# A squared-ReLU MLP on one core: the gate's squares taken from reloaded sums, a third result buffer, and operand builds due by their load

## The chip, the cores and the metric

The kernel runs on one core of one Trainium2 chip. The metric is the device time of one execution in microseconds (us), shown as the median of several runs. TensorE (PE) multiplies, VectorE (DVE) and ScalarE (ACT) work on elements, GpSimd (POOL) and SyncE (SP) mostly issue DMA transfers here. Each engine executes its own instructions in the order in which the program emits them, and waits where an instruction needs something that is not ready.

## The reference

One decoder layer on 512 prompt rows and 64 sample rows (8 sequences of 8), 576 rows in all; D_MODEL is 2048, D_FF 8192. An input projection feeds attention and a convolution, whose outputs go through an output projection; then the second part, which the change is about:

```python
def finish_layer(x, attn, conv_y, pe, g_attn_out, w_out, g_mlp, w_up, w_down, g_ple, w_ple, w_ple_gate):
    B, L = x.shape[0], x.shape[1]
    attn = rms_norm(attn, g_attn_out.reshape(N_HEADS, HEAD_DIM)).reshape(B, L, ATT_WIDTH)
    x = x + jnp.concatenate([attn, conv_y], axis=-1) @ w_out
    hid = jnp.square(jax.nn.relu(rms_norm(x, g_mlp) @ w_up))
    x = x + hid @ w_down
    gate = jax.nn.sigmoid(rms_norm(x, g_ple) @ w_ple_gate)
    return x + (pe @ w_ple) * gate
```

`rms_norm` divides a row by the root of the mean of its squares and multiplies by a gain. The sums run over 2048 features, which lie across the partitions here, so each norm needs the squares of the whole row before its factor is known. A last norm gives the output.

## The kernel before

Phase 1 (projection, attention, convolution) and the output projection (L495) fill the first 1067.7 us and stay as they are but for the last steps. Phase 2 works in float32 by splitting each operand into a high and a low part and multiplying high by high, high by low and low by high.

**Quads and segments.** The unit of the MLP is a quad: a 256 x 256 block of weights against 256 features of 576 rows. Seven products stand for the eight of a 2 x 2 block product (`PRODS`), each of three matmuls of 128 x 288: 21 matmuls, at L1528 (high by high), L1529 (high by low) and L1530 (low weights by high). The seven sums of an output build up in seven of the eight PSUM banks over a *segment*, a run of quads on one output p. At its end a combine makes the four result blocks: `combine_head` (L1637 and L1640 on ACT, L1638 and L1639 on DVE) and, one quad later in the program, `combine_tail` (L1650 to L1653 on DVE). The next segment needs the banks that these release. The result tile is c.

The order is: 32 up segments u0 to u31 of 8 quads; then the 8 outputs of the down product in 5 rounds, d0.0 to d7.4 (output, round), of 3, 3, 3, 4, 5, 6, 7, 8 quads in round 0, 7 each in rounds 1 to 3, and 8, 8, 8, 7, 6, 5, 4, 3 in the last; then the gate, without the seven products: 12 matmuls a quad and row half (L1589 to L1591), first output 0 for both halves (8 quads), then outputs 1 to 7 for each half.

**Weights.** For each quad `QStream.prep` makes w2h (ACT, L149) and w2l (DVE, L152) out of w2r, which a DMA on SP loads and whose sums of blocks DVE makes (L1735 to L1737). It is called two quads ahead; there are three buffers of each.

**Operands.** Down operand k is the squared, rectified result u_k, stored in DRAM (`di`) by `fin_up` and loaded into one of 8 ring slots (`xs`) by `mk`, as soon as the slot's last reader has run. The load is issued by POOL (L1453). Then `slot` splits the loaded tile into high (ACT, 128 x 864 and 128 x 1152) and low parts (DVE, the same shapes). This is called a build below.

**Down results.** Parts of a down output are added in DRAM: `fin_down` issues an accumulating DMA of c onto x1 (L1346, POOL). The last part takes another way: x1 is loaded into `rp` by SP, DVE adds it (L1349), the sum is stored as x2 (L1351), and its squares (ACT L1269, DVE L1276) go into acc, whose sum over the partitions (L179 on PE) gives the gate's norm. Gate operands are loaded from x2 (`xs<-x`) and split with the gain in 128 x 576 pieces.

**What sets the order.** A Python class, `Beside`, weaves this side work into the quads. It holds two queues of generators and a credit; after each quad `run` adds a quad's duration to the credit and steps the heads of the queues until the credit is used up. A yield of a positive number costs so much credit, one of -n means not before n quads from now. `flush` finishes an item regardless. Hooks run the loads at quad positions that are worked out ahead.

Of the kernel before, what the change touches and what calls it, by code (L numbers as in the profile page):

```python
# [18 lines left out]
NR = 576  # L19
NPR = 512  # L20
HR = 288
# [121 lines left out]
class Kern:  # L143
# [70 lines left out]
    def build(self):  # L214
        tc, nc, a = self.tc, self.nc, self.a
        with ExitStack() as top:
# [5 lines left out]
            self.x2 = [dram.tile([128, 2, NR], F32, name=f"x2_{j}") for j in range(8)]  # L222
# [949 lines left out]
    def outproj(self, gen):  # L1172
# [64 lines left out]
    def plan(self):  # L1237
# [10 lines left out]
        loads = []  # L1248
        for g, p, k0, k1 in segs:
            for k in range(k0, k1, 2):  # L1250
                m = min(2, k1 - k)
                loads.append((wsrc[g][p][:, k:k + m], m, g >= 3))
        self.segs = segs
# [11 lines left out]
    def squares(self, p, x):  # L1265
# [4 lines left out]
        yield 0  # L1270
# [8 lines left out]
    def norm(self, ps):  # L1279

        yield -2
        dg = self.buf("dg")[:, 0, :]
        for _ in self.row_rsqrt(ps, self.aux, dg, self.acc2, self.rb2, 2048.0):
            yield -2

    def operands(self, c, g):

        if g is not None:
# [4 lines left out]
            yield 0  # L1293
# [10 lines left out]
    def fin_out(self, p, c):  # L1304
# [5 lines left out]
        if p in (0, 1, 7):  # L1310
            s = self.xslot() if p < 2 else self.last
            yield from self.split7(s, cg, T)
# [4 lines left out]
        if p == 7:  # L1317
            yield from self.squares(p, c)
            self.bg.add(0, self.norm(self.P_))

    def phase2(self):
# [12 lines left out]
        def fin_up(p, c, r, final):  # L1334
# [4 lines left out]
            yield 0  # L1339
# [3 lines left out]
        def fin_down(p, c, r, final):  # L1343

            if not final:
                nc.gpsimd.dma_start(self.x1[p], c, accum_op=ALU.add)  # L1346
                yield 0
                return
            V(c, c, r, ALU.add)  # L1349
            yield EL(2 * NR)  # L1350
            nc.gpsimd.dma_start(self.x2[p], c)  # L1351
            yield from self.squares(p, c)
            if p == 7:
                bg.add(0, self.norm(self.P_))
# [71 lines left out]
        def gate_rows(p, g):  # L1426

            if g == 3:
                return pairbuf(self.pl[p]), pairbuf(self.x2[p])
            r, o = buf("rp"), (g - 4) * HR  # L1430
            for i, src in enumerate((self.pl[p], self.x2[p])):
# [4 lines left out]
               lambda p, final: pairbuf(self.x1[p]) if final else None,  # L1436
# [5 lines left out]
        def mk(g, j):  # L1442
# [7 lines left out]
            src = (self.up_in, self.down_in, self.x2)[g - 1][j]  # L1450
# [4 lines left out]
            if g < 3:  # L1455
                load()

            def build():
                if g == 3:
                    load()  # L1460
                yield -3 if g == 2 and j >= RING else -2
                if g < 3:
                    yield from self.slot(t)
                    return
                for i in range(2):
                    gv = self.g_ple[:, 2 * j + i:2 * j + i + 1]
                    r = f(h.lo[:, i, :])
                    self.split_hi(h.hi[:, i, :], r, scale=gv)
                    nc.vector.scalar_tensor_tensor(h.lo[:, i, :], r, gv, f(h.hi[:, i, :]), ALU.mult, ALU.subtract)
                    yield EL(NR)  # L1470

            h.work = bg.add(1, build())

        quadlist = [(si, k) for si, sg in enumerate(segs) for k in range(sg[2], sg[3])]
# [23 lines left out]
        prev = before = behind = None  # L1498
        for t, (si, k) in enumerate(quadlist):
            g, p, k0, k1 = segs[si]  # L1500
            if prev:
                pg, ppr, c, r, pfinal, pp_ = prev
                if pg >= 3:
# [6 lines left out]
                fin_of[pg, pp_] = bg.add(int(late), fins[pg](pp_, c, r, pg if pg >= 3 else pfinal), 2 if late else None)  # L1510
                before, behind = behind, fin_of[pg, pp_]
# [7 lines left out]
            if k == k0:  # L1519
                pr = {}  # L1520
            if g >= 3:
                self.plain(pr, hi, lo, s, k == k0, k == k1 - 1, rows_of(g))
            else:
                for (i, ia, ib) in self.PRODS:
                    if k == k0:
                        pr[i] = self.P_()
                    o = pr[i][:, :HR]
                    nc.tensor.matmul(o, hi[:, ia, :], s.hi[:, ib, :], start=(k == k0), stop=False)  # L1528
                    nc.tensor.matmul(o, hi[:, ia, :], s.lo[:, ib, :], start=False, stop=False)  # L1529
                    nc.tensor.matmul(o, lo[:, ia, :], s.hi[:, ib, :], start=False, stop=(k == k1 - 1))  # L1530
            for fn in hooks.get(t, ()):
                fn()
            slow = k0 == 0 and p == 0 and g != 2
# [4 lines left out]
            if g == 1 and p == 0 and 2 <= k + 2 < 7:  # L1538
                bg.flush(slots[1, k + 2].work)
            if k == k1 - 1:  # L1540
                if g != 1 or p:
# [3 lines left out]
                if before:  # L1545
                    bg.flush(before)
                if g >= 3:
                    c = t2.tile([128, 2, NR], F32, name="c", tag="c", bufs=2)
# [62 lines left out]
    def split7(self, s, rp, T):  # L1611
# [3 lines left out]
        for h, l, src, n in ((hi[:, 0, :], lo[:, 0, :], rp[:, 0, :HR], HR), (hi[:, 1:3, :], lo[:, 1:3, :], b2, NR),  # L1615
                             (hi[:, 3:, :], lo[:, 3:, :], T, 2 * NR)):
            self.split_hi(h, src)
            self.split_lo(l, src, h)
            yield EL(n)

# [237 lines left out]
```

## Time and profile before

| | |
|---|---|
| median of 3 runs | 2776.98 us (2773.07 to 2781.45) |
| the profiled execution, time | 2781.63 us |
| its span | 2779.9 us |
| PE busy | 2709.3 us (97%) |
| DVE busy | 2097.5 us (75%) |
| ACT busy | 1211.9 us (44%) |
| POOL busy | 521.8 us (19%) |
| MLP matmuls, three lines of 3584 | 298, 298, 297 ns mean |

Lines of groups read: line, engine, operation, out<-in, shape, count, then busy time and mean ns of one, then the engine's idle time right before them and what ended most of it. Lines of a timeline read: start, duration, engine, line, operation, count, and in brackets the idle time before and its releaser. A matmul's duration overlaps its neighbours'; what counts is the distance of their starts. A DMA's last number is the time from issue to landing.

### The profile page before, as it was taken

Reading aid. Unit: us, or ns where it says so; the run is one execution under the profiler, and the core shown is the slowest. Engines: PE = TensorE matmul, PEld = TensorE weight load, DVE = VectorE, ACT = ScalarE, POOL = GpSimd, SP = SyncE. Lnnn points to the kernel's source line nnn. Section 1 sums busy time; section 2 is a strip of 40 time slices with the busy share of each in tenths; the row PEclk is TensorE's granted clock in tenths of the full one; section 3 lists DMA queues with packets and bytes.
Section 4 is the critical chain, followed back from the end, with each engine's and each line's share of the span. In section 5 each row is a group of like instructions: output and inputs, shape, how many; then the busy total and the mean of one; then the engine's idle time right before and its main releaser. Section 6 shows DMA issues by size and latency. Waiting matters only on the chain.

```text
span 2779.9 us, 57369 instructions
## 1 busy us (share of the span) xinstructions
PE 2709.3 (97%) x22217; PEld 2615.8 (94%) x22217; DVE 2097.5 (75%) x3715; ACT 1211.9 (44%) x1841; POOL 521.8 (19%) x927
## 2 busy tenths in 40 slices
PE   8999999999999999999999999989999999999997
PEld 8988889998888998999999999989999999999997
DVE  5577777766655437888888888888888888888676
ACT  4233334345643324444444444444454444444554
POOL 1177766731100000000000000100000000000010
PEclk9999999999999999999999999989999999999999
DMA  4688888988745445444444444665565656656675
GB/s 152 194 287 292 282 289 291 296 295 301 262 133 201 145 161 203 129 146 148 138 143 143 137 139 141 223 158 166 158 192 145 176 162 173 174 164 201 197 239 173
DMA packets 239316, 538.45 MB, mean 194 GB/s; under 512 B 25825, under 2 KB 26722, under 8 KB 239042
## 3 DMA queue, kind: packets, MB, share of 16 engines
q1 hardware_dynamic: 171394, 329.06, 37.0%
q0 software_dynamic: 34112, 144.75, 16.5%
q10 hardware_dynamic: 33536, 60.96, 6.9%
q8 instruction: 174, 2.85, 0.4%
q14 instruction: 100, 0.82, 0.1%
HBM read 442.67 MB, written 92.01 MB: 192 GB/s over the span
## 4 chain that ended last, share of the span: by engine, by line
PE 66%; DVE 4%; issue 1%; ACT 1%; DMA 0%; DVEq 0%; ACTq 0%; SPq 0%; POOLq 0%
PE P L1529 17%; PE P L1528 17%; PE P L1530 16%; PE U L495 7%; PE P L1591 2%; PE P L1589 2%; PE P L1590 2%; PE U L1126 1%; DVE w2l L152 1%; DVE xs L152 1%; DMA xs<-ui 0%; ACT xs L149 0%; DMA w2r<-in_w_up 0%; ACT w2h L149 0%; DVE w2r L1735 0%
## 5 line engine op out<-in xcount | busy, mean ns | idle before, releaser
L1528 PE MATMUL P<-xs,w2h 128*128 128x288 f32 x3584 | 1069.0, 298 | 22.1 <-DVE c L1638 11.1
L1529 PE MATMUL P<-xs,w2h 128*128 128x288 f32 x3584 | 1068.3, 298 | 3.9 <-DVE xs L152 3.9
L1530 PE MATMUL P<-xs,w2l 128*128 128x288 f32 x3584 | 1064.6, 297 | 2.1 <-DVE w2l L152 2.1
L149 ACT ACTIVATE w2h<-w2r 128x896 fp32r<-128x896 f32 (+1 forms) x632 | 557.1, 889 | 756.5 <-PE P L1529 470.5
L152 DVE TENSOR_TENSOR w2l<-w2r,w2h 128x896 fp32r<-128x896 f32 (+1 forms) x632 | 637.7, 1011 | 188.4 <-ACT w2h L149 186.5
L1528 PEld LDWEIGHTS P<-xs,w2h 128*128 128x128 f32 x3584 | 681.2, 190 | 28.7 <-DVE c L1638 14.1
L1529 PEld LDWEIGHTS P<-xs,w2h 128*128 128x128 f32 x3584 | 681.6, 190 | 5.9 <-DVE xs L152 5.6
L1530 PEld LDWEIGHTS P<-xs,w2l 128*128 128x128 f32 x3584 | 679.2, 190 | 2.8 <-DVE w2l L152 2.8
L495 PE MATMUL U<-xh,whi 128*128 128x288 f32 x1792 | 402.1, 306 | 3.0 <-ACT xh L149 1.5
L495 PE MATMUL U<-xh,wlo 128*128 128x288 f32 x1792 | 385.4, 297 | 1.9 <-DVE wlo L129 1.8
L495 PE MATMUL U<-xl,whi 128*128 128x288 f32 x1792 | 384.9, 296 | 2.1 <-DVE xl L328 2.1
L495 PEld LDWEIGHTS U<-xh,whi 128*128 128x128 f32 x1792 | 289.0, 190 | 24.1 <-issue 17.1
L495 PEld LDWEIGHTS U<-xh,wlo 128*128 128x128 f32 x1792 | 289.3, 189 | 3.1 <-DVE wlo L129 3.1
L495 PEld LDWEIGHTS U<-xl,whi 128*128 128x128 f32 x1792 | 289.1, 189 | 3.1 <-DVE xl L328 3.0
L123 ACT ACTIVATE whi<-wraw 128x512 fp32r<-128x512 f32 x224 | 141.2, 630 | 283.5 <-PE U L495 149.4
L129 DVE TENSOR_TENSOR wlo<-wraw,whi 128x512 fp32r<-128x512 f32 x224 | 160.4, 716 | 103.5 <-ACT whi L123 101.8
L1036 DVE SCALAR_TENSOR_TENSOR y<-ue,cv,y 128x512 f32<-128x512 f32 x240 | 182.9, 762 | 4.2
L1735 DVE TENSOR_TENSOR w2r<-w2r 128x512 f32<-128x512 f32 (+1 forms) x272 | 177.6, 653 | 9.2 <-DMA w2r<-in_w_down 4.8
L1037 POOL TENSOR_SCALAR cvt<-us,cv 128x64 f32<-128x64 f32 x240 | 167.4, 698 | 21.8
L1591 PE MATMUL P<-xs,w2l 128*128 128x288 f32 x512 | 151.1, 295 | 1.2 <-DVE w2l L152 1.0
L1589 PE MATMUL P<-xs,w2h 128*128 128x288 f32 x512 | 151.9, 297 | 0.0
L1590 PE MATMUL P<-xs,w2h 128*128 128x288 f32 x512 | 150.8, 295 | 0.0
(378 smaller groups left out, 2980.1 us busy)
## 6 DMA issues: line engine op xcount, KB each, us to landing
k<-in_cache_kv SPq DMA_DIRECT2D x256, 256.0 KB, 4.9
v<-in_cache_kv SPq DMA_DIRECT2D x256, 256.0 KB, 4.8
w2r<-in_w_up SPq DMA_DIRECT2D x128, 512.0 KB, 4.0
w2r<-in_w_down SPq DMA_DIRECT2D x112, 512.0 KB, 4.0
wraw<-in_w_main ACTq DMA_DIRECT2D x156, 256.0 KB, 4.9
xs<-di POOLq DMA_DIRECT2D x32, 1008.0 KB, 6.2
w2r<-in_w_gate SPq DMA_DIRECT2D x60, 512.0 KB, 4.5
x<-c POOLq DMA_DIRECT2D x48, 576.0 KB, 6.9
```

The costliest lines, as they stand in the source:

```text
L149: self.nc.scalar.activation(out, in_, AF.Copy, **kw)
L152: self.nc.vector.tensor_tensor(out, in_, f(hi), ALU.subtract)
L495: self.nc.tensor.matmul(u[:, r, :HR], w, x[:, r * HR:(r + 1) * HR], start=first and n == 0, stop=last and n == 2)
L1036: nc.vector.scalar_tensor_tensor(y, ue[:, j:j + NPR], w, y, ALU.mult, ALU.add)
L1037: nc.gpsimd.tensor_scalar(t, us[:, :, j:j + 8], w, None, ALU.mult)
L1528: nc.tensor.matmul(o, hi[:, ia, :], s.hi[:, ib, :], start=(k == k0), stop=False)
L1529: nc.tensor.matmul(o, hi[:, ia, :], s.lo[:, ib, :], start=False, stop=False)
L1530: nc.tensor.matmul(o, lo[:, ia, :], s.hi[:, ib, :], start=False, stop=(k == k1 - 1))
L1589: nc.tensor.matmul(o, hi[:, ia, :], s.hi[:, kh, rows], start=first and kh == 0, stop=False)
L1590: nc.tensor.matmul(o, hi[:, ia, :], s.lo[:, kh, rows], start=False, stop=False)
L1591: nc.tensor.matmul(o, lo[:, ia, :], s.hi[:, kh, rows], start=False, stop=last and kh == 1)
L1735: lambda: V(w[:, :, 4:6, :], w[:, :, 0:1, :].broadcast_to([128, m, 2, 128]), w[:, :, 1:3, :], ALU.add),
```

## The change

Six things change, all in phase 2 and the steps around it:

1. *Sums in DRAM to the end.* x2 is gone. The last part of a down output is accumulated onto x1 too; the load of x1 and DVE's add go. The gate's operands are loaded from x1, and the squares and their sums are made in the gate operand's build, from the loaded tile; the norm follows the build of operand 7.
2. *A third c.* Three result buffers instead of two; the memory comes from `rx`, which shares a tile with the combine's t5. Result rows r of the gate load into free ring units.
3. *When a build may start.* Before, the wait of 2 or 3 quads began when the build reached its queue's head; now it counts from the load.
4. *Last quad of a segment.* `wait` in place of `run`: the credit is set, but no side work is emitted ahead of the combine.
5. *Spread steps.* Several yields of 0 become -1, so that the next step comes a quad later; fin_up(31) gets a queue of its own that is stepped by `nudge`.
6. *Start of the up stage.* The first weights are loaded three output tiles earlier and their sums made ahead; u0 takes its operands in the order 0, 1, 7, 2, 3, 4, 5, 6 (operand 7 comes straight out of SBUF).

```diff
@@ outproj
-                self.oc_ = t2.tile([128, 2, NR], F32, name="c", tag="c", bufs=2)
-            self.rx = t2.tile([128, NR], F32, name="rx", tag="rx", bufs=1)
+                self.oc_ = t2.tile([128, 2, NR], F32, name="c", tag="c", bufs=3)
+            self.rx = self.w2.tile([128, NR], F32, name="rx", tag="t5", bufs=1)
...
-                if n == KT - 1 and h == 0:
+                if n == KT - 4 and h == 0:
                     for i in range(4):
                         self.W.dma(i)
+                if n == KT - 3 and h % 2:
+                    bg.spend(self.W.ahead(h // 2))
@@ plan
+            parts = [(k, min(2, k1 - k)) for k in range(k0, k1, 2)]
+            if (g, p) == (1, 0):
+                parts = [(0, 2), (7, 1), (2, 2), (4, 2), (6, 1)]
...
@@ fin_down
-            if not final:
-                nc.gpsimd.dma_start(self.x1[p], c, accum_op=ALU.add)
-                yield 0
-                return
-            V(c, c, r, ALU.add)
-            yield EL(2 * NR)
-            nc.gpsimd.dma_start(self.x2[p], c)
-            yield from self.squares(p, c)
-            if p == 7:
-                bg.add(0, self.norm(self.P_))
+            nc.gpsimd.dma_start(self.x1[p], c, accum_op=ALU.add)
+            yield 0
@@ mk
-            if g < 3:
-                load()
+            load()
+            t0 = bg.now
 
             def build():
-                if g == 3:
-                    load()
-                yield -3 if g == 2 and j >= RING else -2
+                wait = t0 + (2, 2, 3 if j >= RING else 2, 4)[g] - bg.now
+                if wait > 0:
+                    yield -wait
                 if g < 3:
                     yield from self.slot(t)
                     return
+                sq = buf("sq2")
+                nc.scalar.activation(sq, f(h.lo), AF.Square)
...
+                if j < 7:
+                    yield -1
+                acc = self.acc2
...
+                if j == 7:
+                    self.found = bg.add(0, self.norm(self.P_, 0))
@@ phase2, in the loop over quads
-            if k == (k1 - 2 if g < 4 else 5) and not slow:
-                bg.flush_all(0)
+            if i == (n - 2 if g < 4 else 4) and not slow:
+                if 1 < g < 4:
+                    bg.flush_all(0)
                 r = pre[g](p, lastseg[g, p] == si)
-            bg.run(1000 + t, (2.79, 3.18, 1.59, 1.59)[max(g - 2, 0)])
...
+            if i == n - 1:
+                bg.wait(1000 + t, dt)
+            else:
+                bg.run(1000 + t, dt)
...
+    def wait(self, t, dt):
+        self.now = t
+        self.credit = min(max(self.credit, -3.0) + dt, dt)
```

In the order of instructions this shows at three places. The first is d7.1, on ACT: L1637/L1640 (L1673/L1676 after the change) are the combine of the segment before, w2h the weights of quad 2 and on, and xs<-xs the two pieces of a build. Before:

```order
L1637 ACTIVATE c<-P 128x288
L1640 ACTIVATE t_25727<-P 128x288
L149 ACTIVATE w2h<-w2r 128x896 x4
L149 ACTIVATE xs<-xs 128x864
L149 ACTIVATE xs<-xs 128x1152
L149 ACTIVATE w2h<-w2r 128x896 x3
L149 ACTIVATE xs<-xs 128x864
L149 ACTIVATE xs<-xs 128x1152
L1637 ACTIVATE c<-P 128x288
```

and after, on the same engine at the same segment:

```order
L1673 ACTIVATE c<-P 128x288
L1676 ACTIVATE t_25724<-P 128x288
L149 ACTIVATE w2h<-w2r 128x896 x3
L149 ACTIVATE xs<-xs 128x864
L149 ACTIVATE xs<-xs 128x1152
L149 ACTIVATE w2h<-w2r 128x896
L149 ACTIVATE xs<-xs 128x864
L149 ACTIVATE xs<-xs 128x1152
L149 ACTIVATE w2h<-w2r 128x896 x3
L1673 ACTIVATE c<-P 128x288
```

The first build stands one weight split earlier, and the second three: the weights of quads 5 and 6 now stand behind a build each, and no build stands directly ahead of the combine. DVE has the low parts (w2l, and xs 864 and 1152) in the same new places.

The second place is the start of the up stage, on ACT. cg is operand 7's result tile times its gain, and xs<-cg and xs<-T are the high parts of operand 7; xs<-xs are those of operands 2, 3 and on, which are loaded. Before:

```order
L149 ACTIVATE w2h<-w2r 128x896 x3
L1291 ACTIVATE cg<-c,vecs 128x576 x2
L149 ACTIVATE xs<-cg 128x288
L149 ACTIVATE xs<-cg 128x576
L149 ACTIVATE xs<-T 128x1152
L149 ACTIVATE xs<-xs 128x864
L149 ACTIVATE xs<-xs 128x1152
```

and after:

```order
L149 ACTIVATE w2h<-w2r 128x896 x3
L1297 ACTIVATE cg<-c,vecs 128x576 x2
L149 ACTIVATE xs<-xs 128x864
L149 ACTIVATE xs<-xs 128x1152
L149 ACTIVATE xs<-xs 128x864
L149 ACTIVATE xs<-cg 128x288
L149 ACTIVATE xs<-cg 128x576
L149 ACTIVATE xs<-T 128x1152
```

The high parts of operand 7, which quad 2 of u0 now uses, stand behind three pieces of operands 2 and 3.

The third place is the end of d7.4 and the gate's first quads, on ACT. sq is the square for the norm, xs<-xs,vecs a gate operand's high parts with the gain, the 128x512 w2h the gate's weights, and rb the norm's factor spread over the partitions. Before:

```order
L1637 ACTIVATE c<-P 128x288
L1640 ACTIVATE t_31023<-P 128x288
L149 ACTIVATE w2h<-w2r 128x512 x2
L1269 ACTIVATE sq_31097<-c 128x1152
L149 ACTIVATE xs<-xs,vecs 128x576
L149 ACTIVATE w2h<-w2r 128x512
L149 ACTIVATE xs<-xs,vecs 128x576
L149 ACTIVATE w2h<-w2r 128x512 x2
L149 ACTIVATE xs<-xs,vecs 128x576 x2
L149 ACTIVATE w2h<-w2r 128x512
L189 ACTIVATE rb_12907<-P 128x512
```

and after:

```order
L1673 ACTIVATE c<-P 128x288
L1676 ACTIVATE t_30993<-P 128x288
L149 ACTIVATE w2h<-w2r 128x512
L1472 ACTIVATE sq_31039<-xs 128x1152
L149 ACTIVATE xs<-xs,vecs 128x576 x2
L149 ACTIVATE w2h<-w2r 128x512 x3
L1472 ACTIVATE sq_31133<-xs 128x1152
L149 ACTIVATE xs<-xs,vecs 128x576 x2
L149 ACTIVATE w2h<-w2r 128x512 x2
L189 ACTIVATE rb_12899<-P 128x512
```

The last two squares read the reloaded tiles xs (of operands 6 and 7) instead of c, and operand 7's stands three weight splits behind operand 6's. On PE the norm's sum (L179) stands behind the gate's fourth quad in both.

More of the change, by code (lines that the diff above doesn't have):

```diff
@@ L1277, in squares, with norm @@
                 yield EL(NR)
-    def norm(self, ps):
-        yield -2
+    def norm(self, ps, wait=2):
+        if wait:
+            yield -wait
         dg = self.buf("dg")[:, 0, :]
@@ L1317, in fin_out, with fin_rows @@
         if p == 7:
-            yield from self.squares(p, c)
-            self.bg.add(0, self.norm(self.P_))
+            self.bg.add(0, self.fin_rows(c))
+    def fin_rows(self, c):
+        yield from self.squares(7, c)
+        yield from self.norm(self.P_)
     def phase2(self):
@@ L1509, in phase2 @@
                 late = (pg, pp_) == (1, 31)
-                fin_of[pg, pp_] = bg.add(int(late), fins[pg](pp_, c, r, pg if pg >= 3 else pfinal), 2 if late else None)
-                before, behind = behind, fin_of[pg, pp_]
+                fin_of[pg, pp_] = bg.add(2 if late else 0, fins[pg](pp_, c, r, pg if pg >= 3 else pfinal))
+                recent.append(fin_of[pg, pp_])
                 prev = None
@@ L1609, in tsums, with split7 @@
         yield 0.74
-    def split7(self, s, rp, T):
+    def split7(self, s, rp, T, spread):
         hi, lo = s[:, 0], s[:, 1]
@@ L1617, in split7 @@
             self.split_hi(h, src)
+            if spread:
+                yield -1
             self.split_lo(l, src, h)
             yield EL(n)
+            if spread:
+                yield -1
     def slot(self, s):
@@ L1692, in run @@
         while self.credit > 0:
-            ready = [q[0] for q in self.q if q and q[0][1] <= t]
+            ready = [q[0] for q in self.q[:2] if q and q[0][1] <= t]
             if not ready:
@@ L1738, in sums, with ahead @@
         return self.EL(m * 256) + 2 * self.EL(m * 128)
+    def ahead(self, l):
+        cost = self.sums(l)
+        self.some(3)
+        return cost
     def some(self, n):
```

101 lines of the change are left out of this document (62 added, 39 removed).

## The prediction

> **What bounds the kernel now.** I read the page's groups of instructions first, then the busy time by stage, then the order of time around each stop of TensorE.
>
> ```profile
> L1528 PE MATMUL P<-xs,w2h 128*128 128x288 f32 x3584 | 1069.0, 298 | 22.1 <-DVE c L1638 11.1
> L1529 PE MATMUL P<-xs,w2h 128*128 128x288 f32 x3584 | 1068.3, 298 | 3.9 <-DVE xs L152 3.9
> L1530 PE MATMUL P<-xs,w2l 128*128 128x288 f32 x3584 | 1064.6, 297 | 2.1 <-DVE w2l L152 2.1
> ```
>
> TensorE is the bound in the MLP: 28.1 us of idle time before 10,752 matmuls. The longest share is the wait for the combine at a segment's border (L1638).
>
> ```profile
> 1067.70:1151.20 83.50, 75.71 (x521) 72.88 (x520) 71.04 (x114) 41.93 (x50) 6.39 (x12) 0.94 0.50 169
> 1151.20:1800.80 649.60, 649.60 (x4874) 649.60 (x4874) 557.99 (x873) 306.49 (x352) 50.44 (x94) 1.00 0.45 147
> 1800.80:1905.80 105.00, 95.22 (x653) 92.94 (x653) 91.01 (x147) 47.41 (x59) 7.43 (x10) 0.92 0.59 163
> 1905.80:2065.40 159.60, 159.60 (x1199) 159.60 (x1199) 138.54 (x217) 74.81 (x89) 11.52 (x16) 1.00 0.62 174
> 2065.40:2401.50 336.10, 333.03 (x2501) 331.56 (x2501) 287.00 (x454) 153.89 (x183) 23.72 (x33) 1.00 0.62 174
> 2401.50:2553.20 151.70, 144.15 (x1031) 141.52 (x1030) 130.49 (x203) 66.46 (x86) 7.83 (x14) 0.97 0.53 166
> 2553.20:2762.00 208.80, 207.61 (x1558) 206.21 (x1558) 142.51 (x255) 109.09 (x187) 26.03 (x39) 1.00 0.66 211
> ```
>
> Columns: stretch, its length, then busy time of PE, PEld, DVE, ACT, POOL, the granted clock, the DMA share. The second row holds 29 up segments of 8 quads: 649.60 / 232 = 2.80 us a quad with nothing lost. By 2.80 the others lose: first three up segments (24 quads) 16.3; first down round (31) 18.2; d7.0 to d6.1 (57) nothing; d7.1 to d7.3 (119) 2.9; last round (49 quads) 14.5; the gate, 1,536 matmuls at 2.80/21, 4.0. Sum 56: the most that any edit of this order can win.
>
> ```profile
> 2245.01 0.40 PE L1528 MATMUL P<-xs,w2h 128*128 128x288 f32 x1 [1.60 <-DVE c L1638]
> 2405.41 0.61 PE L1528 MATMUL P<-xs,w2h 128*128 128x288 f32 x1 [2.36 <-DVE c L1638]
> 2405.81 0.44 PE L1529 MATMUL P<-xs,w2h 128*128 128x288 f32 x1
> 2411.33 0.43 PE L1528 MATMUL P<-xs,w2h 128*128 128x288 f32 x1
> ```
>
> A stop costs more than its length. After 2.36 us idle, 23 matmuls start 5.52 us apart in all, 0.24 each, against 2.80/21 = 0.133: 2.5 us more. After a stop beyond 2 us I add 2.4. The Trainium skill, "TensorE: Matmul & The Clock Gate", Part 1: The HAM clock gate, has half clock after an idle window of about 3.4 us; here 2.36 us was enough, and the measurement decides. By that page the three stops near 3 us priced below would cost 2.4 less each, an estimate 7 us under my sum.
>
> **Down stage, rounds 0 to 3.** Removed: builds that stand directly ahead of the combine. At d7.1, d7.2 and d7.3 the second build's two DVE splits delay the next segment (the two stops above are of this kind). Gain: the 2.9 of the table, and at 2401.5 the stop of 2.36 with its slow matmuls, 5.6. Together 8.5.
>
> Added: the build now stands one weight split earlier on ACT, and the second of a segment three. ACT and DVE work in order, so a build whose load has not landed holds the weights behind it.
>
> ```profile
> 2068.88 0.56 POOL L1453 DMA_DIRECT2D xs<-di  x1 [18.17 <-issue]
> 2069.65 0.85 POOL L1346 DMA_DIRECT2D x<-c  x1 [0.21 <-issue]
> 2071.68 0.56 POOL L1453 DMA_DIRECT2D xs<-di  x1 [1.18 <-issue]
> ```
>
> ```profile
> xs<-di POOLq DMA_DIRECT2D x1, 1008.0 KB, 9.8
> ```
>
> ```profile
> L1453 POOL DMA_DIRECT2D xs<-di x24: 552/560/563, 1909.0 to 2388.2; - x24
> ...
> DMA to landing us min/median/max: 5.7/6.1/10.8
> ```
>
> ```profile
> 2071.09 0.96 ACT L149 ACTIVATE w2h<-w2r 128x896 fp32r<-128x896 f32 x1 [1.84 <-PE P L1529]
> 2075.09 1.98 ACT L149 ACTIVATE xs<-xs 128x864 fp32r<-128x864 f32 x2 [0.23 <-DMA xs<-di]
> 2083.16 1.97 ACT L149 ACTIVATE xs<-xs 128x864 fp32r<-128x864 f32 x2
> ```
>
> ```profile
> L152 DVE TENSOR_TENSOR w2l<-w2r,w2h 128x896 fp32r<-128x896 f32 x255 | 277.3, 1088 | 79.5 <-ACT w2h L149 79.2
> L152 DVE TENSOR_TENSOR xs<-xs 128x1152 fp32r<-128x1152 f32 x30 | 40.6, 1355 | 0.0
> L152 DVE TENSOR_TENSOR xs<-xs 128x864 fp32r<-128x864 f32 x30 | 31.6, 1054 | 1.8 <-ACT xs L149 1.5
> ```
>
> ```profile
> L149 ACT ACTIVATE w2h<-w2r 128x896 fp32r<-128x896 f32 x254 | 241.3, 952 | 364.4 <-PE P L1529 246.1 <-DVE w2r L1737 89.5 <-PE P L1530 10.6
> ```
>
> The times of issue and on ACT are of d7.1, which starts at 2065.4; 9.8 is the landing of its second load, 5.7/6.1/10.8 those of all 24 loads of these rounds; then the mean durations by shape. POOL issues its loads at +3.5 and +6.3 in both kernels, with an accumulating store between them. The second takes 9.8 us and lands at 2081.5. Before, its build came at 2083.16, behind everything; now ACT reaches it at about 2077. From 2081.5: two splits of about 1.0 each on ACT, then the held w2h 0.95, to 2084.5. On DVE the two low parts end at 2084.9 (1.05 and 1.35, the second after ACT), a weight sum about 0.4, w2l 1.09: 2086.3. PE needs that w2l for quad 6, at 2065.4 + 6 x 2.80 + 0.27 = 2082.4. A stop of 3.9, with the slow clock 6.3; I take 6. Three such segments, and d7.0, whose three builds stand in the same manner: 24. Bounds: 0 if the load lands by 2077.8; 30, at 7.5 each, if slow matmuls last as long as behind the stop of 2405 and the landing is 1 later (the largest, 10.8).
>
> The 17 segments with one build: the load lands at +3.5 + 6.1 = +9.6, ACT is free at +6.7 and waits. Low parts and w2l then end at +14.2, and quad 5 wants it at 5 x 2.80 + 0.27 = +14.3. No slack is left: every landing later than 6.2 costs its excess (the largest is 10.8, of a second load). I take 2.5 for the few such; bounds 0 and 17 x 0.7 = 12, if each landed a sixth of the way from 6.1 to 10.8 later (an estimate). Net of this stage: -8.5 + 24 + 2.5 = +18.
>
> **Start of the up stage.**
>
> ```profile
> 1075.56 1.98 ACT L149 ACTIVATE xs<-xs 128x864 fp32r<-128x864 f32 x2 [2.90 <-DMA xs<-ui]
> 1078.29 1.96 ACT L149 ACTIVATE xs<-xs 128x864 fp32r<-128x864 f32 x2
> ```
>
> ```profile
> 1076.53 0.40 PE L1528 MATMUL P<-xs,w2h 128*128 128x288 f32 x1 [2.22 <-ACT xs L149]
> ```
>
> Operand 7 is to be used third, since it needs no load. But its splits now stand on ACT behind those of operands 2 and 3, which wait for loads that let ACT start at 1075.56 and 1078.29. DVE's sums for it follow at about 1081.5, and its last part is ready near 1083, where PE stood from 1074 to 1076.5. The remaining quads find their operands ready, so u0 ends some 3.5 later. u1 and u2 lose 6.8 of the 16.3; a third buffer of c, the earlier weights and squares out of the way should return 5. Net -1.5; bounds -4.5 (the quad order helps) and +6 (no return).
>
> **Up to down.** DVE is busy 91.0 of 105.0 us, so its work bounds this stretch. One build more lies in u31 now (three against two), 2.4 us of DVE less behind it, and fin_up(31) is spread; against that the first build waits for its load. Net -2.5; bounds -8 and +3.
>
> **Last round and gate start.** Removed: eight adds on DVE (L1349, 1.35 each, 10.8 in all), eight loads of x1 on SP, and the squares' wait for them. DVE is busy 130.5 of 151.7 us there, so with this work gone I let all of today's loss go: 14.5, less the 5.6 already counted, + 4.0 = 12.9. The gate's result rows r now load into ring slots from POOL: they are wanted at plain_end, a whole segment later, and cost nothing. The additions, 8 accumulating stores where 8 plain ones were, sit on the path of the squares, which now read the reloaded sum.
>
> ```profile
> DMA to landing us min/median/max: 5.5/8.6/10.1
> ```
>
> ```profile
> xs<-x POOLq DMA_DIRECT2D x1, 576.0 KB, 4.1
> ```
>
> ```profile
> L1269 ACT ACTIVATE sq<-c 128x1152 f32<-128x1152 f32 x8 | 9.3, 1168 | 21.0 <-DVE c L1349 21.0
> L1276 DVE TENSOR_TENSOR acc<-acc,sq 128x576 f32<-128x576 f32 x12 | 9.1, 755 | 5.0 <-ACT sq L1269 4.9
> L1349 DVE TENSOR_TENSOR c<-c,rp 128x1152 f32<-128x1152 f32 x7 | 9.5, 1352 | 0.0
> ```
>
> ```profile
> 2556.97 0.76 DVE L1653 TENSOR_TENSOR c<-c,t 128x576 f32<-128x576 f32 x1
> 2560.89 1.55 DVE L1276 TENSOR_TENSOR acc<-acc,sq 128x576 f32<-128x576 f32 x2 [0.69 <-ACT sq L1269]
> ```
>
> ```profile
> 2566.22 1.17 PE L179 MATMUL P<-ones,acc 128*128 128x2 f32 x10
> ```
>
> The first line is the landing of the accumulating store (L1346), the second that of the last reload before; then durations, and the gate's start in order of time. In the last norm, L179 stands after gate quad 4 in both kernels, at 2566.2. Now c is ready at 2557.7, the sum lands 5.5 behind an issue at about 2558.0, at 2563.5, the reload, with POOL's 0.56 to issue, 4.7 later at 2568.2, square 1.17 and two adds 1.5: 2570.9. PE stops 4.6, with the slow clock 7. Before, the adds ended at 2562.4 and hid; that cover is gone. In d3.4, d4.4 and d5.4 the same chain, counted from the preceding segment's end E: sum ready E + 2.8, stored by E + 9, reloaded by E + 14. ACT arrives at E + 9.5 and holds a weight split that PE needs at E + 17.1; square, two scaled copies, w2h, and on DVE two adds, two low parts and w2l bring it to about E + 20. Three stops near 3, with the clock 5 each: 15. With 7 for the norm and 2 for the gate's other waits (half of today's 4.0) that is 24. Net +11; bounds -5 (only the norm's 7 and 1 more are left) and +20 (the three stops 7 each, the norm 10 with a landing of 8.6).
>
> **The sum.** +18 - 1.5 - 2.5 + 11 = +25. The profiled execution took 2781.6, so about 2806.6; it stands 4.65 above the median of the three runs, 2776.98 (2773.07 to 2781.45), and against that I predict 2802. Other stages are unchanged row for row.
>
> **Rivals.** *Faster, about 2755.* All loads land about 6 us after issue, as lone ones do: then the second lands at +12.5, its weight split is ready at 2082.4, exactly when wanted, and the 24 and 2.5 go. Gained are 8.5, 4.5 and 5 at the two other borders, and 5 in the last round: -23, against 1 for lone late loads. For it: the lone loads' median of 6.1; against it: the 9.8 is measured with the same store in between. It decides at a landing of +12.5.
> *About the same, 2778.* The stops in the down stage go as above, but the chain of the last round stays at its price: -8.5 + 2.5 - 1.5 - 2.5 + 11 = +1.
> *Much slower, about 2827.* The 17 lone builds stop PE as well: 17 x 0.7 = 12, the second loads cost 30, and the last round +20: 12 + 30 - 8.5 + 20 - 1.5 - 2.5 = +50. Against it: landings at 6.1 leave these builds just in time.
> *The change doesn't do what it says.* Operand 7 third is such a case, and is in the sum.
>
> **Chances.** The forecast 0.64, between +9 and +43 (its own range 2786 to 2820). Much slower 0.13, same 0.11, faster 0.12. Within 0.3%, 8.3 us, a measurement of this kernel can't tell a change. Slower: 0.77; same 0.11; faster 0.12. The range holds the forecast, the same case and half of the much slower: 2768 to 2828.
>
> **What would show it.** Right: PE stops of 3 to 4 us before L1555 (w2l) some 17 us into d7.0 to d7.3, ACT idle before xs for DMA xs<-di near 3 us in each segment; no L1674 wait at borders of rounds; a PE stop before L179 of 4 to 5 us; u0 longer than 31.9 us. Wrong: xs<-di landing by +12.5 in d7.1, so that these stops are missing, or matmuls at 0.133 right behind a stop of 3 us.

## The result, and the profile after

| | before | after |
|---|---|---|
| median | 2776.8 us (2773.07 to 2781.45, 4 runs) | 2817.95 us (2808.72 to 2826.49, 4 runs) |
| ratio to before | 1 | 1.0146, 95% interval 1.013 to 1.0163 |
| profiled execution | 2781.63 us | 2826.49 us |
| its span | 2779.9 us | 2824.7 us |

The change makes the kernel 41 us slower by the medians and 45 us by the two profiled executions. 2802 was forecast, with a range of 2768 to 2828.

Busy time by stage of the kernel after (stretch, its length, then PE, PEld, DVE, ACT, POOL, granted clock, DMA): u31 and the first seven segments of the down stage; the stretch from the start of d7.0 to the end of d7.3, rounds 1 to 3 with it; the last round; the gate.

```profile
1776.60:1901.80 125.20, 115.52 (x821) 112.69 (x820) 111.52 (x178) 61.49 (x75) 12.83 (x20) 0.96 0.66 194
1901.80:2431.50 529.70, 510.73 (x3699) 501.13 (x3698) 426.44 (x673) 226.58 (x274) 35.31 (x49) 0.98 0.59 163
2431.50:2587.40 155.90, 145.10 (x1032) 143.46 (x1031) 117.75 (x191) 65.16 (x83) 10.23 (x14) 0.95 0.53 134
2587.40:2807.00 219.60, 211.52 (x1560) 209.85 (x1559) 142.29 (x256) 109.71 (x186) 27.55 (x41) 0.98 0.63 199
```

The second row is 176 quads, 492.8 us at 2.80 a quad: 36.9 are lost. In the kernel before, the same quads lost 2.9. The gate took 208.8 from its first matmul to the start of the tail, now 219.6.

To compare kernels, the matmuls are counted off in each trace: the start of a segment is that of its first matmul, and what a segment takes beyond 2.80 per quad is its loss. A comparison of whole executions would mix in the stages ahead: u0 starts at 1067.7 before, at 1066.0 after, and at 1059.2 to 1071.1 in the runs below.

| lost, us | before | after |
|---|---|---|
| u0 to u3 | 16.2 | 16.2 |
| u31 and d0.0 to d6.0 | 18.2 | 16.0 |
| the four segments d7.0 to d7.3 (second loads) | -0.2 | 26.9 |
| the four segments d0.1 to d0.4 (the borders behind them) | 9.5 | 0.2 |
| the other segments of rounds 1 to 3 | -0.8 | 9.6 |
| d1.4 to d7.4 | 9.1 | 18.7 |
| gate | 4.2 | 14.9 |

From the start of u0 to the gate's last matmul the losses differ by 46.5 us (46.3 by the rounded rows); less 1.7 for the earlier start of u0 they make the 45 us.

Where the waits now end, from the page's groups on PE:

```profile
L1553 PE MATMUL P<-xs,w2h 128*128 128x288 f32 x3584 | 1075.0, 300 | 31.8 <-ACT w2h L149 12.7
L1555 PE MATMUL P<-xs,w2l 128*128 128x288 f32 x3584 | 1070.1, 299 | 12.6 <-DVE w2l L152 12.4
L1554 PE MATMUL P<-xs,w2h 128*128 128x288 f32 x3584 | 1070.6, 299 | 3.5 <-DVE xs L152 3.5
```

The combine (L1638, 11.1 us before) has given up the first place to the weights: 12.7 on w2h, and 12.4 on w2l against 2.1 before. What made the weights late stands in ACT's groups. First of the kernel before, then of the one after:

```profile
L149 ACT ACTIVATE xs<-xs 128x864 fp32r<-128x864 f32 x37 | 34.0, 918 | 6.6 <-DMA xs<-di 3.3 <-DMA xs<-ui 2.9
```

```profile
L149 ACT ACTIVATE xs<-xs 128x864 fp32r<-128x864 f32 x37 | 34.1, 922 | 77.9 <-DMA xs<-di 72.2 <-DMA xs<-ui 4.6 <-PE P L1555 1.1
L1472 ACT ACTIVATE sq<-xs 128x1152 f32<-128x1152 f32 x8 | 9.3, 1163 | 27.2 <-DMA xs<-x 27.2
```

ACT stands 72.2 us in front of down builds whose load is on its way, 3.3 before; and 27.2 us in front of the gate's squares. In d7.1, which starts at 2073.1, on POOL (a load, the accumulating store, the second load), on ACT and on PE, and the landing of the second load, from its issue at 2080.11:

```profile
2077.06 0.56 POOL L1459 DMA_DIRECT2D xs<-di  x1 [21.12 <-issue]
2077.61 0.90 POOL L1354 DMA_DIRECT2D x<-c  x1
2080.11 0.56 POOL L1459 DMA_DIRECT2D xs<-di  x1 [1.61 <-issue]
```

```profile
2083.04 1.99 ACT L149 ACTIVATE xs<-xs 128x864 fp32r<-128x864 f32 x2 [2.63 <-DMA xs<-di]
2084.93 0.94 ACT L149 ACTIVATE w2h<-w2r 128x896 fp32r<-128x896 f32 x1
2089.40 1.98 ACT L149 ACTIVATE xs<-xs 128x864 fp32r<-128x864 f32 x2 [3.54 <-DMA xs<-di]
2091.29 0.93 ACT L149 ACTIVATE w2h<-w2r 128x896 fp32r<-128x896 f32 x1
```

```profile
2092.27 0.40 PE L1553 MATMUL P<-xs,w2h 128*128 128x288 f32 x1 [1.82 <-ACT w2h L149]
2094.43 0.61 PE L1555 MATMUL P<-xs,w2l 128*128 128x288 f32 x1 [1.63 <-DVE w2l L152]
```

```profile
xs<-di POOLq DMA_DIRECT2D x1, 1008.0 KB, 9.3
```

The second load lands at 2089.4, 16.3 us into the segment. The weights of quad 6 (w2h at 2091.29) stand behind the second build, which starts at 2089.40 as its load lands. PE waits first for the high part, then for the low part, 3.45 us together. The norm's stop on PE, with what precedes it on DVE (first) and the reload of operand 7 (last):

```profile
2606.16 1.55 DVE L1484 TENSOR_TENSOR acc<-acc,sq 128x576 f32<-128x576 f32 x2 [4.28 <-ACT sq L1472]
```

```profile
2607.76 2.30 PE L179 MATMUL P<-ones,acc 128*128 128x2 f32 x10 [6.76 <-DVE acc L1484]
```

```profile
xs<-x POOLq DMA_DIRECT2D x1, 576.0 KB, 6.5
```

### The profile page after: what moved, and what is told of

Read it like the earlier page. It is cut to its first block, busy times and chain, and to the rows that moved or that the text cites. A ratio compares the mean times of both kernels' runs of the same rounds, so it can differ in the third digit from the quotient of the medians.

```text
span 2824.7 us, 57303 instructions
## 1 busy us (share of the span) xinstructions
PE 2728.3 (97%) x22217; PEld 2625.1 (93%) x22217; DVE 2082.6 (74%) x3710; ACT 1208.8 (43%) x1841; POOL 527.1 (19%) x929
## 4 chain that ended last, share of the span: by engine, by line
PE 46%; issue 7%; DMA 3%; DVE 3%; ACT 1%; POOL 0%; DVEq 0%; ACTq 0%; POOLq 0%
PE P L1553 13%; PE P L1555 13%; PE P L1554 13%; DMA xs<-di 3%; PE P L1621 2%; PE P L1623 2%; PE P L1622 2%; DVE w2l L152 1%; ACT xs L149 0%; DMA xs<-x 0%; DVE xs L152 0%; ACT w2h L149 0%; DMA x<-c 0%; DVE w2r L1780 0%; POOL x L1354 0%
## 5 line engine op out<-in xcount | busy, mean ns | idle before, releaser
L1553 PE MATMUL P<-xs,w2h 128*128 128x288 f32 x3584 | 1075.0, 300 | 31.8 <-ACT w2h L149 12.7
L1555 PE MATMUL P<-xs,w2l 128*128 128x288 f32 x3584 | 1070.1, 299 | 12.6 <-DVE w2l L152 12.4
L1555 PEld LDWEIGHTS P<-xs,w2l 128*128 128x128 f32 x3584 | 682.9, 191 | 17.8 <-DVE w2l L152 17.1
L494 PEld LDWEIGHTS U<-xh,whi 128*128 128x128 f32 x1792 | 288.2, 189 | 23.6 <-issue 16.9
```

The costliest lines, as they stand in the source:

```text
L494: self.nc.tensor.matmul(u[:, r, :HR], w, x[:, r * HR:(r + 1) * HR], start=first and n == 0, stop=last and n == 2)
L1553: nc.tensor.matmul(o, hi[:, ia, :], s.hi[:, ib, :], start=(i == 0), stop=False)
```

## The experiments

Each was timed against the kernel before on the same chip; what it lost, stage by stage, is read from its one profiled execution. "d7.0 to d7.3" and "d0.1 to d0.4" are the four segments each of the table. The theory: builds are due before their loads land, and ACT and DVE hold weight splits behind them. The rival: the new order has pushed too much of DVE's work into these quads.

**Down builds due later.**

```diff
-                wait = t0 + (2, 2, 3 if j >= RING else 2, 4)[g] - bg.now
+                wait = t0 + (2, 2, 5 if j >= RING else 2, 4)[g] - bg.now
```

> The changed kernel with one number altered: a down build is due 5 quads after its load instead of 3. My theory (ACT holds weight splits behind loads that have not landed): the load has landed whenever ACT reaches the build, so the stops in d7.0 to d7.3 (27 us in the trace) and the small ones of the lone builds (some 8) go: 2818 becomes about 2785. The rival (the new rule for the last quad has pushed too much of DVE's work into the quads between, and the stops are DVE's own): the same work stands in the same segment, so the stops stay in another quad and the time is within 8 us of 2818.

Measured: 2796.43 us, ratio 1.0077 (1.006 to 1.0094), so 21 less than the kernel after. d7.0 to d7.3 lose 0.2 in place of 26.9 and the other segments 1.6 in place of 9.6: the stops were the loads'. But the borders d0.1 to d0.4 lose 10.1 again, where after lost 0.2 and before 9.5. With 5 quads a segment's second build starts 17.5 us into d7.1, close to the combine, as before the change (17.8). That is most of the difference to 2785.

**This rule alone, in the kernel before.**

```diff
-            if g < 3:
-                load()
+            if g < 3:
+                load()
+            t0 = bg.now
 
             def build():
                 if g == 3:
                     load()
-                yield -3 if g == 2 and j >= RING else -2
+                    yield -2
+                else:
+                    wait = t0 + (3 if g == 2 and j >= RING else 2) - bg.now
+                    if wait > 0:
+                        yield -wait
```

> The kernel before with this one part of the change: the wait of a down build counts from its load. My theory: the stops of d7.0 to d7.3 appear here too (24 to 27), with some 8 for lone builds, and the builds ahead of the combine go (8.5 gained): 2777 becomes about 2800. The rival (they come of the whole, DVE's work in the quads between): without the other parts it stays within 8 us of 2777.

Measured: 2809.28 us, ratio 1.012 (1.0103 to 1.0137). By the medians the one rule costs 33 us, more than the 24 expected. d7.0 to d7.3 lose 25.5, the other segments 6.8, the borders only 0.8. All its losses together are 24 above those of the kernel before; the profiled execution was the fastest of four, 2801.38, and where the median's further 8 lie is not known. So this rule alone makes both the loss and the gain at the borders; the third c and the last quad's rule are needed for neither.

**The last part sums as before, in the kernel after.**

```diff
-            nc.gpsimd.dma_start(self.x1[p], c, accum_op=ALU.add)
-            yield 0
+            if not final:
+                nc.gpsimd.dma_start(self.x1[p], c, accum_op=ALU.add)
+                yield 0
+                return
+            V(c, c, r, ALU.add)
+            yield EL(2 * NR)
+            nc.gpsimd.dma_start(self.x2[p], c)
+            yield from self.squares(p, c)
+            if p == 7:
+                self.found = bg.add(0, self.norm(self.P_))
...
-                sq = buf("sq2")
-                nc.scalar.activation(sq, f(h.lo), AF.Square)
```

> The changed kernel with the last part sums as before: x1 loaded, added on DVE, stored as x2, squares from c; all else as changed. My theory (the chain accumulate, reload, square holds ACT and the norm): the 18.8 us lost in d3.4 to d6.4 and the 6.8 before L179 fall to about the 9 and 0 of before, so 2818 becomes about 2800. The rival (the last round loses by DVE's work and the third buffer, whoever makes the squares): within 8 us of 2818.

Measured: 2809.02 us, ratio 1.0108 (1.0088 to 1.0127): 9 gained in place of 18. The gate's loss falls from 14.9 to 6.2, as expected of the norm. d1.4 to d7.4 still lose 16.0. Half of my theory of the last round fell: most of the cost stays with plain stores. In this run's groups on ACT the wait has only moved from the square to the gate operand's high part, which needs the same reload:

```profile
L149 ACT ACTIVATE xs<-xs,vecs 128x576 fp32r<-128x576 f32 x16 | 11.5, 766 | 15.1 <-DMA xs<-x 15.1
```

**Gate builds due later.** The new theory: the gate's builds, too, stand before their load, whichever way the sum was made.

```diff
-                wait = t0 + (2, 2, 3 if j >= RING else 2, 4)[g] - bg.now
+                wait = t0 + (2, 2, 3 if j >= RING else 2, 6)[g] - bg.now
```

> The changed kernel, but a gate operand's build is due 6 quads after its load's issue instead of 4. After the run with the squares put back, which left 16.0 of 18.7 in d3.4 to d6.4, two causes are open there. Theory: ACT again holds weight splits behind a reload, whatever makes the squares; with two quads more the reload has landed, the 18.7 fall to 10 or less, and with the norm's stop halved 2818 becomes about 2805. The rival (DVE's work at these short segments, with squares and builds, is the bound): the 18.7 stay within 3.

Measured: 2796.63 us, ratio 1.007 (1.0046 to 1.0093): 21 gained, where 13 were expected. The last round's and the gate's row:

```profile
2426.00:2566.50 140.50, 137.98 (x1031) 136.14 (x1030) 118.04 (x192) 65.12 (x83) 10.22 (x14) 1.00 0.58 148
2566.50:2776.50 210.00, 208.33 (x1559) 206.35 (x1558) 142.42 (x255) 109.82 (x186) 27.53 (x41) 1.00 0.67 208
```

```profile
L1472 ACT ACTIVATE sq<-xs 128x1152 f32<-128x1152 f32 x8 | 9.2, 1151 | 0.0
```

ACT's wait for the reload ahead of the square is 0.0, and the last round loses 3.3, less than the 9.1 before the change; the gate 5.4. Two quads more were enough. DVE's work in these stretches is the same as after (118.0 and 117.8 us), so it was not what made those stops.

**The sums in DRAM alone, in the kernel before.**

```diff
-            if not final:
-                nc.gpsimd.dma_start(self.x1[p], c, accum_op=ALU.add)
-                yield 0
-                return
-            V(c, c, r, ALU.add)
-            yield EL(2 * NR)
-            nc.gpsimd.dma_start(self.x2[p], c)
-            yield from self.squares(p, c)
-            if p == 7:
-                bg.add(0, self.norm(self.P_))
+            nc.gpsimd.dma_start(self.x1[p], c, accum_op=ALU.add)
+            yield 0
...
                 yield -3 if g == 2 and j >= RING else -2
                 if g < 3:
                     yield from self.slot(t)
                     return
+                yield from self.squares(j, f(h.lo))
+                if j == 7:
+                    bg.add(0, self.norm(self.P_, 0))
```

> The kernel before with this one part of the change: the last part sums are accumulated in DRAM, and squares taken from the reloaded gate operand. My theory: d3.4 to d7.4 lose 5 to 10 more than the 9.1 of before, since ACT waits for accumulate and reload ahead of the square, and L179 waits 3 to 7 us: 2776 becomes about 2788. The rival (DVE loses eight adds of 1.35 us, and the last round is bound by DVE): the last round gets shorter and the time falls below 2772.

Measured: 2815.68 us, ratio 1.013 (1.0109 to 1.015): 39 slower, three times what I expected. The last round loses 30.7 and the gate 24.0. Here a gate build stands 2 quads behind its load's issue, not 4. ACT's wait for the reloads, and the three longest stops of PE from d6.4 into the gate:

```profile
L1269 ACT ACTIVATE sq<-xs 128x1152 f32<-128x1152 f32 x8 | 9.3, 1163 | 37.5 <-DMA xs<-x 37.5
```

```profile
2542.57 0.61 PE L1524 MATMUL P<-xs,w2h 128*128 128x288 f32 x1 [5.38 <-ACT w2h L149]
2562.25 0.40 PE L1524 MATMUL P<-xs,w2h 128*128 128x288 f32 x1 [3.97 <-ACT c L1633]
2582.07 0.61 PE L1585 MATMUL P<-xs,w2h 128*128 128x288 f32 x1 [7.21 <-ACT c L1633]
```

Set beside the 9.1 of the kernel before, the last round with sums in DRAM loses 22 more at 2 quads (30.7), 10 more at 4 (18.7, the kernel after) and 6 less at 6 (3.3). That is the place of the build, not the price of the sums: at 4 quads the old sums lose 16.0. The run at 2 quads lacks the other parts of the change, too.

**What delays the second load.** Rounds 0 to 3 add nothing to x1 here.

```diff
-            nc.gpsimd.dma_start(self.x1[p], c, accum_op=ALU.add)
+            if final:
+                nc.gpsimd.dma_start(self.x1[p], c, accum_op=ALU.add)
```

> The changed kernel without the accumulating stores of rounds 0 to 3, so that the output lacks these parts of the down product; loads, builds and matmuls are the same. If the store that runs between two loads is what delays the second: it lands some 6 us after issue, the stops in d7.0 to d7.3 fall from 27 to under 8. If it is the first load, of 1008 KB, that holds the second in the queue: 9 to 10 us still, and the stops stay at 24 to 27.

Measured (a single execution): 2796.82 us. The landing of the second load of d7.1 and the median of the 24 loads:

```profile
xs<-di POOLq DMA_DIRECT2D x1, 1008.0 KB, 5.6
```

```profile
xs<-di POOLq DMA_DIRECT2D x24, 1008.0 KB, 5.2
```

5.6 us in place of 9.3, and d7.1 to d7.3 lose 1.1 in place of 19.7, the other segments, most of them with one lone build, nothing (-1.7 in place of 9.6). The borders lose 4.2 in place of 0.2, which is not explained. d7.0 keeps 4.2: its three loads follow one another, and the second and third take 8.6 and 8.3 us even so. So with no accumulating store between the two loads the second lands early at d7.1 to d7.3, and the moment of landing decides; a load close ahead delays one as well, as d7.0 shows. The second load now lands at +11.6, and the new order is harmless, as the forecast's rival said of a landing by +12.5.

**First and second build apart.** nth counts the loads of one segment: its first build is due 4 quads after its load, every later one 8.

```diff
+            sg = quadlist[t0 - 999][0] if t0 > 999 and g == 2 and j >= RING else None
+            nth = loads_of.get(sg, 0)
+            loads_of[sg] = nth + 1
...
-                wait = t0 + (2, 2, 3 if j >= RING else 2, 4)[g] - bg.now
+                wait = t0 + (2, 2, (8 if nth else 4) if j >= RING else 2, 4)[g] - bg.now
```

> The changed kernel, but the first build of a down segment is due 4 quads after its load and the second 8, which puts the second into the next segment, behind its combine. My theory as the run with 5 quads left it (stops come of loads that have not landed, border stops of a build that stands too near to the combine): neither is left, so d7.0 to d7.3 lose under 2 us, the segments behind them under 2 in place of 10, and 2818 becomes about 2785. The rival (two builds in a stretch cost DVE some 10 us wherever they stand): the borders behind d7.r or the segments after lose the 10 again, about 2796 as with 5 quads.

Measured: 2780.83 us, ratio 1.0016 (0.9994 to 1.0038), 37 less than the kernel after. The stretch from the start of d7.0 to the end of d7.3:

```profile
1901.70:2394.50 492.80, 492.80 (x3699) 492.80 (x3698) 425.09 (x670) 228.25 (x272) 35.31 (x49) 1.00 0.62 175
```

PE is busy in all of it, and 492.8 is 176 quads at 2.80: nothing is lost in it. The busy times of DVE and ACT (425.1 and 228.3) are those of after (426.4 and 226.6), so the rival is out: the work was there all along, and only its place was wrong.

**u0 in order.**

```diff
-            if (g, p) == (1, 0):
-                parts = [(0, 2), (7, 1), (2, 2), (4, 2), (6, 1)]
```

> The changed kernel with u0's operands in the order 0 to 7 again. My theory (operand 7 third waits behind the splits of 2 and 3): u0's loss falls from 11.5 to about 9, so 2818 becomes about 2815, at the edge of what can be told. The rival (operand 7 third is what saves time there, since it needs no load): u0 gets longer and 2818 becomes 2822 or more.

Measured: 2814.65 us, ratio 1.0133 (1.0116 to 1.015), against 1.0146 after: by the time alone no difference can be told. By the trace u0 loses 8.9 in place of 11.5, u0 to u3 13.0 in place of 16.2. By that one trace operand 7 third costs 3 us.

**The cures together.** Down builds at 4 and 8 quads, gate builds at 6, u0 in order: the edits above in one kernel.

> The changed kernel with the three cures together: down builds due 4 and 8 quads after their loads, gate builds 6, and u0's operands in the order 0 to 7. If the losses are apart as the single runs have them (up start 13.0, up to down 16.5, down borders 0.7, last round 3.3, gate 5.4: 39 against the 57 of before), it takes 18 less than before: about 2758. If the cures share a loss, it stays above 2766.

Measured: 2762.22 us against 2774.54, ratio 0.9942 (0.9923 to 0.996): 12 less than before by the medians, 16 by the ratio. The losses are 12.8 (u0 to u3), 16.9 (u31 and d0.0 to d6.0), 0.9 (from there to the end of d0.4), 3.4 (the rest of the last round) and 6.0 (the gate), 40 in all, as the single runs had them (39). The kernel before lost 56: 9.0 of the 16 are the borders, 5.7 the last round and 3.4 the start of the up stage. Which of the third c, the earlier weights and the spread steps gave the last was not tried.

**The same, with the first builds later.**

```diff
-                wait = t0 + (2, 2, (8 if nth else 4) if j >= RING else 2, 6)[g] - bg.now
+                wait = t0 + (2, 2, (8 if nth else 4) if j >= RING else 4, 6)[g] - bg.now
```

> The same as the run with the three cures, and the first down builds (operands 0 to 7, loaded in u31) due 4 quads after their loads instead of 2. One theory: u31's stop of 2.9, where ACT waits for the first load, goes and nothing comes back: 3 less than the run beside it. The other: DVE is the bound from u31 to d5.0, so a later start comes back in d0.0 to d2.0: within 3 of it, or above.

Measured: 2755.89 us, ratio 0.9921 (0.9897 to 0.9944), the best of all. The intervals of this and the run beside it overlap; by the traces u31 loses 0.0 in place of 3.1 and the stretch to d6.0 14.3 in place of 16.9, so the stop of u31 was not DVE's and most of it does not come back. Another 3.6 us between the two traces are the down stage from d7.0 to the end of d7.3, where the quads of rounds 2 and 3 ran at 2.77 us instead of 2.80 (see the end); why is open.

**The cures, with the sums as before the change.** The edit of the third experiment in the kernel with the cures.

> The run with the three cures, but the last part sums as before the change (load x1, add on DVE, store x2, squares from c). It asks what the sums in DRAM are worth where no build waits for its load. If they save DVE's work in the last round: this run is 3 to 8 longer than the run with the cures. If the shorter chain to the squares is worth more: it is shorter.

Measured: 2767.37 us, ratio 0.9966 (0.995 to 0.9982) against 0.9942: the time can't tell them apart. The last round loses 9.7 in place of 3.4. So by the traces the sums in DRAM are worth some 6 us there once no build waits for its load.

## Why the prediction came out as it did

*Down stage.* Right in mechanism and place. The four segments with several builds were priced at 24 and lose 26.9; the stop in d7.1 was worked out as 3.9 and, with the slow clock, 6.3, and measures 3.45 and 6.5. The borders were to give 8.5 and gave 9.3. The term that was too small is that of the lone builds: 2.5 taken, 10.4 measured (9.6 against -0.8). The working counted 17 such segments; there are 15, since 24 builds less 3 in d7.0 and 2 each in d7.1 to d7.3 leave 15. It had found no slack at a landing of 6.1, which is the median of all 24 loads and not of the lone ones alone, and then charged only the few late ones. The trace shows a loss of 0.3 to 0.6 in nine of these segments, some 4 us in all, and 5.8 in three with later loads: 3.0 in d6.1, where the load took 8.5, and 1.4 each in d5.2 and d4.3. A place with no slack pays for all of the spread, and the bound of 12 was nearer than the value taken.

*Last round and gate.* +11 taken, +20 measured, at the bound. The norm's stop was worked out as 4.6 and is 6.76: the reload takes 6.5, not 4.1. That 4.1 was the shortest of the eight reloads before the change, and not the last of them:

```profile
DMA to landing us min/median/max: 4.1/5.3/7.6
```

The loads of the gate's result rows are issued right behind the reload now, and I had costed these at nothing. Whether they make it late is open: with the same two loads behind it the reload took 4.0 in the run with the old sums and 4.8 in that with down builds at 5 quads. The whole gate was to lose 9 (7 for the norm, 2 for its other waits) and loses 14.9. d3.4, d4.4 and d5.4 were priced at 15 and lose 14.8; d6.4, which was not priced, loses 4.0 more. Most of the loss of before would have gone, as taken: at 6 quads the last round loses 3.3 in place of 9.1. The step that failed is the cause given for the stops: "the additions, 8 accumulating stores where 8 plain ones were, sit on the path of the squares". With plain stores 16.0 stay, and with the accumulating ones and two quads more 3.3. The cause is the same as in the down stage, a build that is due before its load has landed.

*Start of the up stage.* u0 was to end some 3.5 later for operand 7, and loses 2.0 more; undone, it gains 2.6. u1 and u2 were to return 5; they return 2.4, so the stage stays at 16.2 where 1.5 was expected to be gained. The earlier start of u0, 1.7, is within what the runs scatter there.

*Up to down.* -2.5 taken, -2.2 measured. The wait of the first build for its load shows as u31's 2.9, and costs 3 that can be had back. The other 13.1, in d0.0 to d6.0, were put down to DVE's work; no run settles that.

*The sum.* +25 taken, +45 in the profiled executions, +41 in the medians: of the miss of 20 against the profiled execution, 10 are in the down stage (8 of them the lone builds), 9 in the last round and the gate.

*The rivals.* Faster needed the second load to land at +12.5. It lands at +16.3, and decides as said: with the parts left out it lands at +11.6, and the stops go. That the change does not do what it says held for operand 7.

*The slow clock.* 2.4 was added to each stop beyond 2 us. After the stops of d7.0 to d7.3 and of the last round, 14 to 23 matmuls start 0.24 apart, 0.11 more than 2.80/21 each: 1.5 to 2.5. So the price taken was near the upper end, and 2 us is no border (more on that at the end). The stop in d6.4 was 1.96; five matmuls at full speed follow it, and then, from 2567.56 to 2571.00, 14 slow ones:

```profile
2566.37 0.40 PE L1553 MATMUL P<-xs,w2h 128*128 128x288 f32 x1 [1.96 <-ACT c L1673]
```

The Trainium skill, "TensorE: Matmul & The Clock Gate", Part 1: The HAM clock gate, asks for an idle window of about 3.4 us; the 1.96 here is shorter, and so is every stop of d7.0 to d7.3 (the longest is 2.72). The same section says that the window runs freely and that the count of slow matmuls varies; the varying counts and the late beginning here agree with that.

## What to carry to other kernels

On engines that work in order, a step that waits for a transfer belongs behind the moment when the transfer lands, not behind that when it was issued, with room for the spread of the landings; everything that stands behind it in the queue is late by as much. Count the landing where it happens, with the other transfers of the queue in between: 9.3 us here, where the same load takes 5.6 without the accumulating stores. A change of several parts can hide a gain behind one number: this one is 1.5% slower as written and 0.6% to 0.8% faster with its builds due at the right quads and u0 in order.

## What the runs showed of the hardware

- *The length of a stop alone does not tell whether the clock falls.* In d7.1 two stops of 1.82 and 1.63 us, with two matmuls between them, are followed by slow matmuls: from 2094.84 to 2099.88 they start 0.24 apart, then 0.13. The granted clock of the stretch from 2096 to 2100 is 0.50 (behind POOL's figure in the first row).

```profile
2096.00:2100.00 4.00, 4.00 (x18) 4.00 (x18) 3.54 (x6) 2.52 (x5) 0.00 (x0) 0.50 0.13 47
2092.51 0.29 PE L1554 MATMUL P<-xs,w2h 128*128 128x288 f32 x1
2099.64 0.44 PE L1555 MATMUL P<-xs,w2l 128*128 128x288 f32 x1
2100.10 0.30 PE L1554 MATMUL P<-xs,w2h 128*128 128x288 f32 x1
2100.24 0.29 PE L1555 MATMUL P<-xs,w2l 128*128 128x288 f32 x1
```

Two stops of 0.92 and 1.23 in d6.1 were followed by matmuls 0.13 apart. In the kernel before, a stop of 1.46 us in d5.0, six matmuls behind one of 0.37, was followed by 12 slow matmuls; in the best run, a stop of 2.43 in d0.0 was followed by none (granted clock 1.00). Their lines:

```profile
1869.01 0.61 PE L1528 MATMUL P<-xs,w2h 128*128 128x288 f32 x1 [1.46 <-DVE c L1638]
1800.88 0.40 PE L1555 MATMUL P<-xs,w2h 128*128 128x288 f32 x1 [2.43 <-DVE c L1676]
```

- *A quad takes 2.80 or 2.77 us with PE busy throughout.* This is the stretch from the start of d7.0 to the end of d7.3 in the best run, 176 quads:

```profile
1898.20:2387.80 489.60, 489.51 (x3697) 489.11 (x3697) 425.36 (x671) 228.10 (x272) 35.25 (x49) 1.00 0.62 176
```

It is 3.2 us shorter than the row of the run with first and second build apart, with next to no idle time in either. In the kernel before, round 2 ran at 2.77 between two stops and the others at 2.80. What sets it is open; it was not tried.

- *Loads land later beside accumulating stores, the ones ahead of a store too.* In most segments the store is issued some 0.5 us behind the load (2077.06 and 2077.61 above). The 24 loads land after 6.1 us in the median with these stores and, in the single execution without, after 5.2.
